# Mixer A's sink as a further column of a head's scores, and a row's maximum turned in sign by ScalarE, in a two-layer fp32 encoder

## The chip, the cores and the metric

The kernel runs on one core of one Trainium2 chip, as one program. The metric is the device time of one execution in microseconds (us). Five engines matter: TensorE (PE in the profile; its weight loads are listed as PEld), VectorE (DVE), ScalarE (ACT), GpSimd (POOL), and the sync engine (SP), from whose queue every DMA of this kernel is issued.

## The reference

Two layers over 256 tokens of width 2048, all in fp32. Each layer has a mixer sub-layer and a gated MLP with a convolution of width 3. The part that the change touches is the softmax of the mixer's two attentions, 8 heads each of width 128:

```python
# mixer A: window attention with a learned sink per head
s = jnp.where(mask, q @ k.T * HEAD_DIM ** -0.5, NEG_INF)
m = jnp.maximum(jnp.max(s, axis=-1, keepdims=True), snk)
p = jnp.exp(s - m)
p = p / (jnp.sum(p, axis=-1, keepdims=True) + jnp.exp(snk - m))
o = p @ v
# mixer B: neighbourhood attention with a 2-D relative bias, a plain softmax without a sink
p = jax.nn.softmax(s + bias)
```

Around it: `h @ w_in` gives q, k, v and two gates; `w_proj_a` and `w_proj_b` project the heads' outputs; the gated sum goes through `w_out`; then `w_up`, the convolution, silu times value, and `w_down`. An adaLN product (`silu(c) @ ada_w`) gives shifts, scales and gates.

## The kernel before, in words

**Products in three parts.** Every fp32 product is made of three fp32r matmuls: each operand is split into a high part and a rest, and high x high, high x rest, rest x high are summed in PSUM. `feature_block` (L314 to L316) does this for one 128x128 block of weights against 256 tokens: the weights `hl` are stationary, the activations are the moving operand, 256 columns (258 where a `Bare` chunk carries two more columns). `tokens` (L377 to L379) does q, k and v the other way round: activations `h` stationary, 512 columns of `hl` moving.

**The stream of weights.** The weights come in units of 1 MB, 16 blocks, in the order of use. For each unit SP issues a DMA into a `raw` buffer, ACT writes the high part of each half (L297), and DVE the rest (L298), into one of four `hl` buffers. DVE also does the adaLN product, one 128x2048 instruction per 1 MB tile of `ada_w` (L226).

**Attention** runs in the background of that stream. A generator per head is advanced by one step at the end of some units. `head_a` and `head_b` take a buffer `p` (tag "p", two buffers) and call `attend`: PE makes the scores `sc` (L607); for each of two halves of the tokens DVE adds the mask (A) or the bias (B, which a DMA has put into `p` itself) and takes the row maximum `m`, begun at the sink for A (L610); DVE turns the sign (`nm`, L615); ACT takes the exponential with its row sum `den` (L618). For A, ACT then makes exp(sink - max) (`es`, L621) and DVE adds it to `den` (L622). DVE takes the reciprocal (L624), ACT scales the rows (L626), PE transposes them (`tp`, L631), the halves of the transpose go to `pT`, and PE multiplies with `v` (`po`, L639).

**GpSimd** does the inverse square roots alone: of q's and k's norms (`qrs`, L441) and of the layer norms (L457).

**Where tiles lie.** Pools are laid out one after another in a partition of SBUF; in the built programs a tile begins at a multiple of 32 bytes. In order: `const` (with `x`), `lay`, `raw`, `hl`, `h`, `ev`, `at` (the attention's buffers: `qn`, `p`, `pT`, and the halves of v, q and k), `sm` (the small tiles: `m`, `nm`, `den`, `es`, `ri`, three buffers each), a padding of 224 bytes, and last `s`, whose seven places hold, by turns, the packed q, k and v, the heads' outputs `oA` and `oB`, the gates `ya` and `gb`, the bare chunks, and the MLP's activations `act`. So the size of `p` and the number of tags in `sm` set where `s` begins. A few tiles are shifted by the code: with `OFF, ROW = 48, 64` (floats), `chunks_of` puts the last chunk of a place 64 bytes further on where there is room, `led` puts chunk 0 of `h` and of `merged` 192 bytes ahead of the rest's phase, `paired` (heads 6 and 7 of `oA`) shifts by 64 bytes. The "phase" of an operand below is its byte address modulo 256, in the built program.

| operand, before | phase |
|---|---|
| stationary `hl` in L314 to L316 | 32 |
| moving `h`, `merged`: chunk 0; the other 15 | 32; 224 |
| moving `act`, `oA`, `oB`: most chunks | 224 |
| moving, the last chunk of `act` in the second and third groups of the MLP, `oB` of head 7, `oA` of heads 6 and 7 | 32 |
| `pT` and the halves of k (moving); the halves of q and v (stationary) | 224; 32 |

The scheduler orders each engine's instructions by its own estimate of the times, so an edit in `attend` shifts neighbouring work by some places.

Of the kernel before, what the change touches and what calls it, by code (L numbers as in the profile page):

```python
# [9 lines left out]
F32 = mybir.dt.float32  # L10
F32R = mybir.dt.float32r
AF = mybir.ActivationFunctionType
ALU = mybir.AluOpType
AX = mybir.AxisListType

P = 128
L = 2
D = 2048
S = 256
# [115 lines left out]
def encoder(ctx: ExitStack, tc: tile.TileContext, a: dict, out: bass.AP):  # L135
    nc = tc.nc
# [14 lines left out]
    at = pool("at", 2)  # L151
    sm = pool("sm", 3)
# [30 lines left out]
    def place(tag, n, dt, name):  # L183
        return sp.tile([P, n, S], dt, name=name, tag=tag)
# [16 lines left out]
    def paired(dt, name):  # L201

        t = ev.tile([P, 2 * S + ROW], dt, name=name, tag="u", bufs=2)
        return t[:, ROW - OFF : ROW - OFF + 2 * S].rearrange("p (a s) -> p a s", a=2)
# [181 lines left out]
    def split(dst, src, scale=None):  # L386

        if scale is None:
            nc.scalar.copy(dst[:, 0], src)
            nc.vector.tensor_tensor(out=dst[:, 1], in0=src, in1=dst[:, 0].bitcast(F32), op=ALU.subtract)  # L390
            return
        nc.scalar.activation(out=dst[:, 0], in_=src, func=AF.Copy, scale=scale)
        nc.vector.scalar_tensor_tensor(
            out=dst[:, 1], in0=src, scalar=scale, in1=dst[:, 0].bitcast(F32), op0=ALU.mult, op1=ALU.subtract
        )
# [192 lines left out]
    def in_halves(src, name, tag, yes):  # L588

        if not yes:  # L590
            return (src,)
        off = {"vh": ROW - OFF, "qh": 0, "kh": OFF}[tag]
        hl = at.tile([P, 2 * S + off], F32R, name=name, tag=tag, bufs=1)[:, off:]
        halves = hl.rearrange("p (i s) -> p i s", i=2) if len(src.shape) == 2 else hl.rearrange("p (i a s) -> p i a s", i=2, a=2)
        split(halves, src)
        return halves[:, 0], halves[:, 1]

    def by(x):

        return ((0, 0), (0, 1), (1, 0))[: 2 * len(x) - 1]  # L600

    def attend(q, k, v, p, mask, scale, sink, o):

        sc = ax.tile([P, 2, S], F32, name="sc", tag="ax")
        for t in range(2):
            for i, j in by(q):
                nc.tensor.matmul(sc[:, t], q[i][:, t * P : (t + 1) * P], k[j], start=i + j == 0, stop=(i, j) == by(q)[-1])  # L607
        m = sm.tile([P, 2], F32, name="m", tag="m")
        for t in range(2):
            nc.vector.tensor_tensor_reduce(  # L610
                out=p[:, t], in0=sc[:, t], in1=mask[:, t], scale=scale, scalar=-3.0e38 if sink is None else sink,
                op0=ALU.add, op1=ALU.max, accum_out=m[:, t : t + 1],
            )
        nm = sm.tile([P, 2], F32, name="nm", tag="nm")
        nc.vector.tensor_scalar(out=nm[:], in0=m[:], scalar1=-1.0, scalar2=None, op0=ALU.mult)  # L615
        den = sm.tile([P, 2], F32, name="den", tag="den")
        for t in range(2):
            nc.scalar.activation(out=p[:, t], in_=p[:, t], func=AF.Exp, bias=nm[:, t : t + 1], accum_out=den[:, t : t + 1])  # L618
        if sink is not None:
            es = sm.tile([P, 2], F32, name="es", tag="es")  # L620
            nc.scalar.activation(out=es[:], in_=nm[:], func=AF.Exp, bias=sink)  # L621
            nc.vector.tensor_tensor(out=den[:], in0=den[:], in1=es[:], op=ALU.add)  # L622
        ri = sm.tile([P, 2], F32, name="ri", tag="ri")
        nc.vector.reciprocal(out=ri[:], in_=den[:])  # L624
        for t in range(2):
            nc.scalar.activation(out=p[:, t], in_=p[:, t], func=AF.Copy, scale=ri[:, t : t + 1])  # L626
        yield
        tp = ax.tile([P, 2, S], F32, name="tp", tag="ax")
        for k in range(2):
            for t in range(2):  # L630
                nc.tensor.transpose(tp[:, k, t * P : (t + 1) * P], p[:, t, k * P : (k + 1) * P], ident[:])  # L631
        pT = at.tile([P, 2, 2, S], F32R, name="pT", tag="pT", bufs=1)
        split(pT, tp[:])
        v = v()
        yield
        po = ax.tile([P, 512], F32, name="po", tag="ax")
        for i, j in by(v):
            for b in range(2):
                nc.tensor.matmul(po[:, :S], v[i][:, b], pT[:, j, b], start=i + j + b == 0, stop=i + b == 2)  # L639
        o = o()  # L640
        nc.scalar.copy(o[:, 0], po[:, :S])
        nc.vector.tensor_tensor(out=o[:, 1], in0=po[:, :S], in1=o[:, 0].bitcast(F32), op=ALU.subtract)
# [93 lines left out]
    def small(l):  # L736

        if l == 0:
            tables.extend((load(a["maskA"], [P, 2, S], "maskA"), load(a["cs"], [P, 2, 2, HALF], "cs")))
        cs = tables[1]  # L740
        gains = load(a["gains"][l], [P, 4], f"gains{l}", lay, tag="gains", bufs=1)
        rg = load(a["rg"][l], [P, 2, ROT], f"rg{l}", lay, tag="rg", bufs=1)
        sink = load(a["sink"][l], [P, HA], f"sink{l}", lay, tag="sink", bufs=1)
        cw = load(a["cw"][l], [P, 2 * FC, 4], f"cw{l}", lay, tag="cw", bufs=1)
        nc.vector.tensor_scalar(out=gains[:, 2:3], in0=gains[:, 2:3], scalar1=SCALE, scalar2=None, op0=ALU.mult)
        rots = []
        for w in range(2):
            rot = lay.tile([P, 4, 2, HALF], F32, name=f"rot{l}_{w}", tag=f"rot{w}", bufs=1)
            for i, (f, g) in enumerate(((0, 0), (1, 1), (0, 1), (1, 0))):
                nc.vector.tensor_tensor(  # L750
                    out=rot[:, i], in0=cs[:, f],
                    in1=rg[:, w, g * HALF : (g + 1) * HALF].unsqueeze(1).broadcast_to([P, 2, HALF]), op=ALU.mult,
                )
            rots.append(rot)

        return gains, sink, cw, rots

    for l in range(L):
# [41 lines left out]
        def head_a(i):  # L800
            g = i // (HA // GA)
            if i >= 6:
                oA.append(paired(F32R, f"oA{l}_{i}"))
            elif i % 2 == 0:
                o = place(("y0", "y1", "y2")[i // 2], 4, F32R, f"oA{l}_{i}")
                oA.extend((o[:, :2], o[:, 2:]))
            q = in_halves(qTa[:, i], f"qA{l}_{i}", "qh", l in SCORES_3)
            if i % (HA // GA) == 0:
                kvs[0] = in_halves(kTa[:, g], f"kA{l}_{g}", "kh", l in SCORES_3)
            k = kvs[0]  # L810
            yield
            p = at.tile([P, 2, S], F32, name="p", tag="p")

            def v():
                if i % (HA // GA) == 0:
                    kvs[1] = in_halves(packs[0][:, 1:4:2, g * HEAD : (g + 1) * HEAD], f"vA{l}_{g}", "vh", True)
                return kvs[1]

            yield from attend(q, k, v, p, tables[0], SCALE, sink[:, i : i + 1], lambda: oA[i])

        def head_b(hb):
            b, i = packs[1 + hb // 4], hb % 4
            v = b[:, 4:8].rearrange("p (t a) s -> p t (a s)", t=2)
            p = at.tile([P, 2, S], F32, name="p", tag="p")
            nc.sync.dma_start(p[:], a["bias"][l, hb])
            q = in_halves(b[:, 8 + i], f"qB{l}_{hb}", "qh", l in SCORES_3)
            k = in_halves(b[:, i], f"kB{l}_{hb}", "kh", l in SCORES_3)
            yield
            yield from attend(
                q, k, lambda: in_halves(v[:, :, i * HEAD : (i + 1) * HEAD], f"vB{l}_{hb}", "vh", True), p, p, 1.0, None,  # L830
                lambda: oB_of(hb),
            )

        def oB_of(hb):
            if hb == 0:
                o = place("a", 12, F32R, f"oB{l}_{hb}")
                oB.extend(o[:, 2 * i : 2 * i + 2] for i in range(6))
            elif hb == 6:
                oB.extend(chunks_of(sp, "b0", 6, f"oB{l}_{hb}", 2))
            return oB[hb]  # L840
# [30 lines left out]
        for pi, (groups, gates) in enumerate(parts):  # L871
            last = pi == len(parts) - 1
            for g, part in enumerate(groups):
                have_h(part)
                pss = st.tokens(h, part)
                if pi == max(0, len(parts) - 2) and g == 0:
                    gains, sink, cw, rots = small(l)
# [56 lines left out]
        for tag in ("y0", "y1", "y2"):  # L934
            t = place(tag, 4, F32, f"gb{l}_{tag}")
            gb += [t[:, i] for i in range(4)]
        for i in range(2):
            t = paired(F32, f"gb{l}_{i}")
# [207 lines left out]
```

## Time and profile before

| | |
|---|---|
| time, three runs | 2666.4, 2667.25, 2667.46 us; median 2667.25 |
| the profiled execution's own time | 2668.06 us |
| its span (first to last instruction) | 2666.3 us |
| busy: PE / DVE / ACT / POOL | 2654.0 / 2099.9 / 1410.1 / 35.8 us |
| matmuls | 21256 |
| moved by DMA | 700.41 MB |

How to read it: a matmul's own duration (some 277 ns) overlaps the next one's, so busy time says only that PE was never without work. What a stretch costs is read from the starts of its matmuls, or from their count in a window: a matmul that begins before the window's edge is counted too, which adds some 2.4 to the count, since one lasts 276 ns and a new one begins each 113 ns.

### The profile page before, as it was taken

The numbers are of one execution on the slowest core, as the hardware profiler recorded it, in microseconds if no ns is written. First come the engines' busy times: TensorE is split into PE (matmuls) and PEld (weight loads), VectorE is DVE, ScalarE is ACT, GpSimd is POOL, SyncE is SP. The second block draws the span as 40 slices with busy tenths as digits, with TensorE's granted clock in tenths as the row PEclk, the third lists the DMA queues.
The fourth block names the chain that finished last, engine by engine and source line by source line (L and its number), as shares of the span: only waits on it lengthen the run. The fifth ranks groups of instructions, "written<-read, shape, count | busy, mean of one in ns | idle before, by whom it ended". The sixth has DMA issues, their size and how long they took to land.

```text
span 2666.3 us, 50840 instructions
## 1 busy us (share of the span) xinstructions
PE 2654.0 (100%) x21256; PEld 2566.7 (96%) x21256; DVE 2099.9 (79%) x2959; ACT 1410.1 (53%) x2284; POOL 35.8 (1%) x25
## 2 busy tenths in 40 slices
PE   9999999999999999999999999999999999999999
PEld 7888899999999999999998889999999999999999
DVE  8898998997987888788886666768888866655664
ACT  5445864446653554355554566554565445544553
POOL 0001100000000000000000000000000000000000
PEclk9999999999999999999999999999999999999999
DMA  9987779885777878788757666666747775555554
GB/s 365 354 328 292 263 280 357 327 313 204 281 291 296 292 293 294 284 298 288 293 215 254 231 236 225 246 256 247 291 167 292 294 256 193 190 192 194 198 192 143
DMA packets 102039, 700.41 MB, mean 263 GB/s; under 512 B 12721, under 2 KB 15025, under 8 KB 17969
## 3 DMA queue, kind: packets, MB, share of 16 engines
q1 hardware_dynamic: 101810, 697.17, 71.2%
q8 instruction: 166, 2.72, 0.4%
q14 instruction: 63, 0.52, 0.1%
HBM read 695.03 MB, written 2.10 MB: 261 GB/s over the span
## 4 chain that ended last, share of the span: by engine, by line
PE 89%; DVE 6%; DMA 2%; ACT 1%; issue 1%; POOL 0%; SPq 0%; DVEq 0%; ACTq 0%
PE ps L314 25%; PE ps L316 25%; PE ps L315 25%; PE ps_t L379 4%; PE ps_t L377 4%; PE ps_t L378 4%; DVE hl L298 2%; DVE aw L226 2%; DMA aw<-in_aw 1%; PE sc L607 1%; ACT hl L297 1%; PE po L639 1%; DMA w<-in_ws 1%; PE tp L631 1%; PE qtp L580 0%
## 5 line engine op out<-in xcount | busy, mean ns | idle before, releaser
L298 DVE TENSOR_TENSOR hl<-w,hl 128x1024 fp32r<-128x1024 f32 x928 | 1127.6, 1222 | 345.6 <-ACT hl L297 342.4
L297 ACT CAST hl<-w 128x1024 fp32r<-128x1024 f32 x928 | 970.0, 1049 | 719.5 <-PE ps L316 504.7
L314 PE MATMUL ps<-h,hl 128*128 128x256 f32 x3328 | 922.1, 277 | 1.3 <-DVE ya L915 0.6
L315 PE MATMUL ps<-h,hl 128*128 128x256 f32 x3328 | 919.9, 276 | 0.0
L316 PE MATMUL ps<-h,hl 128*128 128x256 f32 x3328 | 919.7, 277 | 0.0
L314 PEld LDWEIGHTS ps<-h,hl 128*128 128x128 f32 x3328 | 624.7, 188 | 2.3 <-DVE ya L915 0.8
L315 PEld LDWEIGHTS ps<-h,hl 128*128 128x128 f32 x3328 | 625.3, 188 | 0.3 <-DVE h L470 0.2
L316 PEld LDWEIGHTS ps<-h,hl 128*128 128x128 f32 x3328 | 624.3, 188 | 0.0
L226 DVE CUSTOM_DVE_ANT_0 aw<-aw,cact,ab 128x2048 f32<-128x2048 f32 x189 | 443.5, 2347 | 73.6 <-DMA aw<-in_aw 73.3
L377 PE MATMUL ps_t<-hl,h 128*128 128x512 f32 x576 | 223.2, 392 | 2.6 <-ACT h L469 1.7
L378 PE MATMUL ps_t<-hl,h 128*128 128x512 f32 x576 | 224.9, 391 | 0.3
L379 PE MATMUL ps_t<-hl,h 128*128 128x512 f32 x576 | 224.4, 390 | 0.0
L991 DVE SCALAR_TENSOR_TENSOR u<-ps,cw,u 128x255 f32<-128x255 f32 x304 | 146.1, 481 | 62.0 <-ACT u L989 58.0
L989 ACT ACTIVATE u<-ps,cw 128x256 f32<-128x256 f32 x152 | 85.6, 563 | 171.5 <-PE ps L316 171.3
L316 PE MATMUL ps<-merged,hl 128*128 128x256 f32 x512 | 141.9, 277 | 0.8 <-DVE hl L298 0.8
L314 PE MATMUL ps<-merged,hl 128*128 128x256 f32 x512 | 141.7, 277 | 0.0
L315 PE MATMUL ps<-merged,hl 128*128 128x256 f32 x512 | 141.6, 277 | 0.0
L315 PE MATMUL ps<-act_o,hl 128*128 128x256 f32 x512 | 141.4, 276 | 0.0
L316 PE MATMUL ps<-act_o,hl 128*128 128x256 f32 x512 | 141.3, 276 | 0.0
L314 PE MATMUL ps<-act_o,hl 128*128 128x256 f32 x512 | 141.2, 276 | 0.0
L377 PEld LDWEIGHTS ps_t<-hl,h 128*128 128x128 f32 x576 | 107.9, 188 | 25.9 <-ACT h L469 2.7
L378 PEld LDWEIGHTS ps_t<-hl,h 128*128 128x128 f32 x576 | 108.1, 188 | 24.1 <-DVE hl L298 2.1
(231 smaller groups left out, 4617.6 us busy)
## 6 DMA issues: line engine op xcount, KB each, us to landing
w<-in_ws SPq DMA_DIRECT2D x463, 1024.0 KB, 4.9
aw<-in_aw SPq DMA_DIRECT2D x189, 1024.0 KB, 6.0
p<-in_bias SPq DMA_DIRECT2D x16, 256.0 KB, 3.3
x<-in_xT SPq DMA_DIRECT2D x4, 512.0 KB, 5.3
aw_o<-in_aw SPq DMA_DIRECT2D x2, 1024.0 KB, 12.3
out<-x SPq DMA_DIRECT2D x16, 128.0 KB, 2.7
w<-in_ws SPq DMA_DIRECT2D x2, 512.0 KB, 11.6
aw_b<-in_aw SPq DMA_DIRECT2D x1, 1024.0 KB, 18.4
```

The costliest lines, as they stand in the source:

```text
L226: nc.vector.tensor_tensor_reduce(out=raw[:], in0=raw[:], in1=cact[:], scale=1.0, scalar=ab[:, i : i + 1], op0=ALU.mult, op1=ALU.add, accum ...
L297: nc.scalar.copy(hl[:, 0], r)
L298: nc.vector.tensor_tensor(out=hl[:, 1], in0=r, in1=hl[:, 0].bitcast(F32), op=ALU.subtract)
L314: nc.tensor.matmul(out, hi, act[0], start=first, stop=False)
L315: nc.tensor.matmul(ps[:, :S], hi, act[1], start=False, stop=False)
L316: nc.tensor.matmul(out, lo, act[0], start=False, stop=last)
L377: nc.tensor.matmul(ps[:], xh, hi, start=kc == kcs[0], stop=False)
L378: nc.tensor.matmul(ps[:], xh, lo, start=False, stop=False)
L379: nc.tensor.matmul(ps[:], xl, hi, start=False, stop=kc == kcs[-1])
L607: nc.tensor.matmul(sc[:, t], q[i][:, t * P : (t + 1) * P], k[j], start=i + j == 0, stop=(i, j) == by(q)[-1])
L989: nc.scalar.activation(out=u, in_=ps, func=AF.Identity, scale=w[:, 1:2], bias=w[:, 3:4])
L991: nc.vector.scalar_tensor_tensor(out=u[:, to], in0=ps[:, of], scalar=w[:, j : j + 1], in1=u[:, to], op0=ALU.mult, op1=ALU.add)
```

## The change

For mixer A, `p` gets one column more, and GpSimd writes the head's sink into it ahead of the scores. The exponential then runs over 257 columns, so that the row sum holds exp(sink - max), and `es` with its addition goes. The maximum's sign is turned by ScalarE (a Copy with scale -1) in all heads, in place of VectorE. `p` of mixer B takes the same, wider buffer, and its bias is loaded into the first 256 columns of each half.

```diff
         for t in range(2):
             nc.vector.tensor_tensor_reduce(
-                out=p[:, t], in0=sc[:, t], in1=mask[:, t], scale=scale, scalar=-3.0e38 if sink is None else sink,
+                out=p[:, t, :S], in0=sc[:, t], in1=mask[:, t, :S], scale=scale, scalar=-3.0e38 if sink is None else sink,
                 op0=ALU.add, op1=ALU.max, accum_out=m[:, t : t + 1],
             )
         nm = sm.tile([P, 2], F32, name="nm", tag="nm")
-        nc.vector.tensor_scalar(out=nm[:], in0=m[:], scalar1=-1.0, scalar2=None, op0=ALU.mult)
+        nc.scalar.activation(out=nm[:], in_=m[:], func=AF.Copy, scale=-1.0)
         den = sm.tile([P, 2], F32, name="den", tag="den")
         for t in range(2):
-            nc.scalar.activation(out=p[:, t], in_=p[:, t], func=AF.Exp, bias=nm[:, t : t + 1], accum_out=den[:, t : t + 1])
-        if sink is not None:
-            es = sm.tile([P, 2], F32, name="es", tag="es")
-            nc.scalar.activation(out=es[:], in_=nm[:], func=AF.Exp, bias=sink)
-            nc.vector.tensor_tensor(out=den[:], in0=den[:], in1=es[:], op=ALU.add)
+            n = S if sink is None else S + 1
+            nc.scalar.activation(
+                out=p[:, t, :n], in_=p[:, t, :n], func=AF.Exp, bias=nm[:, t : t + 1], accum_out=den[:, t : t + 1]
+            )
...
-            nc.scalar.activation(out=p[:, t], in_=p[:, t], func=AF.Copy, scale=ri[:, t : t + 1])
+            nc.scalar.activation(out=p[:, t, :S], in_=p[:, t, :S], func=AF.Copy, scale=ri[:, t : t + 1])
...
-            p = at.tile([P, 2, S], F32, name="p", tag="p")
+
+            p = at.tile([P, 2, S + 1], F32, name="p", tag="p")
+            nc.gpsimd.tensor_copy(out=p[:, :, S], in_=sink[:, i : i + 1].broadcast_to([P, 2]))
...
-            p = at.tile([P, 2, S], F32, name="p", tag="p")
-            nc.sync.dma_start(p[:], a["bias"][l, hb])
+            p = at.tile([P, 2, S + 1], F32, name="p", tag="p")
+            nc.sync.dma_start(p[:, :, :S], a["bias"][l, hb])
```

**What it moves in SBUF.** The two `p` buffers grow from 2048 to 2056 bytes each, rounded up to 2080: 64 bytes more. Everything behind them in `at` and `sm` lies 64 bytes further on. `es` had three buffers of 32 bytes; without them `s` begins 96 bytes earlier, 32 in all. In the built programs:

| tile | byte before | byte after | phase before, after |
|---|---|---|---|
| `pT` (moving) | 152032 | 152096 | 224, 32 |
| halves of v, of q (stationary; v's begin 64 bytes into the tile) | 156128, 158240 | 156192, 158304 | 32, 96 |
| halves of k (moving; 192 bytes into the tile) | 160288 | 160352 | 224, 32 |
| places of `s`: b0, y0, a, o, b1 | 163808, 176096, 188384, 200672, 217056 | 163776, 176064, 188352, 200640, 217024 | 224, 192 |

`raw`, `hl`, `h`, `merged`, `x` and `ev` stay where they were. So all moving chunks that lay at 224 in `s` lie at 192, and the shifted last ones of `act` and `oB` at 0 in place of 32; `oA` of heads 6 and 7, in `ev`, stays at 32.

**What it moves in the queues.** DVE in the first two heads of layer 0, before (`sc`, `p`, `m`, `nm`, `den`, `es`, `ri` as above; `sink_996` is layer 0's sink; the ISA rows of L610 are the maximum, those of L226 the adaLN product; `rot` is a table for the next layer):

```order
298 L610 ISA m 128x1
299 L610 ISA p,m<-sc,maskA,sink_996 128x256
300 L610 ISA m 128x1
301 L298 TENSOR_TENSOR hl_45_1_2472<-w_45_2467,hl_45_1_2472 128x1024
302 L615 TENSOR_SCALAR nm<-m 128x2
303 L556 TENSOR_TENSOR qn<-packB_0_224,qrs 128x512 x2
304 L226 ISA aw_37_2640,mod_172<-aw_37_2640,cact,ab_173 128x2048
305 L226 ISA mod_172 128x1
306 L622 TENSOR_TENSOR den<-den,es 128x2
307 L750 TENSOR_TENSOR rot_0_15957<-cs,rg_15950 128x32 x2
308 L624 RECIPROCAL ri<-den 128x2
309 L298 TENSOR_TENSOR hl_46_0_2538<-w_46_2536,hl_46_0_2538 128x1024
```

And after:

```order
298 L610 ISA m 128x1
299 L610 ISA p,m<-sc,maskA,sink_996 128x256
300 L610 ISA m 128x1
301 L298 TENSOR_TENSOR hl_45_1_2470<-w_45_2465,hl_45_1_2470 128x1024
302 L556 TENSOR_TENSOR qn<-packB_0_224,qrs 128x512 x2
303 L226 ISA aw_37_2634,mod_172<-aw_37_2634,cact,ab_173 128x2048
304 L226 ISA mod_172 128x1
305 L623 RECIPROCAL ri<-den 128x2
306 L298 TENSOR_TENSOR hl_46_0_2534<-w_46_2532,hl_46_0_2534 128x1024
```

`nm` and the addition to `den` are gone from DVE's queue, where `nm` stood behind an L298; the table `rot` has moved elsewhere, and the rest is in the same order.

GpSimd's queue from the first layer norm on, before:

```order
10 L457 TENSOR_TENSOR nrs<-ms_in,mhalf 128x2
11 L441 TENSOR_TENSOR qrs<-qss,mhalf 128x4
12 L441 TENSOR_TENSOR qrs<-qss,mhalf 128x8 x6
13 L457 TENSOR_TENSOR nrs<-nss,mhalf 128x2 x2
14 L441 TENSOR_TENSOR qrs<-qss,mhalf 128x4
15 L441 TENSOR_TENSOR qrs<-qss,mhalf 128x8 x6
```

And after (`sink_996` and `sink_15936` are the sinks of the two layers):

```order
10 L457 TENSOR_TENSOR nrs<-ms_in,mhalf 128x2
11 L813 COPY p<-sink_996 128x2 x2
12 L441 TENSOR_TENSOR qrs<-qss,mhalf 128x4
13 L441 TENSOR_TENSOR qrs<-qss,mhalf 128x8 x3
14 L813 COPY p<-sink_996 128x2 x2
15 L441 TENSOR_TENSOR qrs<-qss,mhalf 128x8
16 L813 COPY p<-sink_996 128x2
17 L441 TENSOR_TENSOR qrs<-qss,mhalf 128x8
18 L813 COPY p<-sink_996 128x2 x2
19 L441 TENSOR_TENSOR qrs<-qss,mhalf 128x8
20 L813 COPY p<-sink_996 128x2
21 L813 COPY p<-sink_15936 128x2 x2
```

The copies of the sink stand among the inverse roots of q's and k's norms; from row 14 on a root stands behind copies that need a `p` buffer to be free.

## The prediction

> **What bounds the kernel now.** I read the page first (busy time, clock, chain), then PE in windows of a single stage, then single matmul starts, and last the two attentions.
>
> ```profile
> span 2666.3 us, 50840 instructions
> PE 2654.0 (100%) x21256; PEld 2566.7 (96%) x21256; DVE 2099.9 (79%) x2959; ACT 1410.1 (53%) x2284; POOL 35.8 (1%) x25
> PEclk9999999999999999999999999999999999999999
> PE 89%; DVE 6%; DMA 2%; ACT 1%; issue 1%; POOL 0%; SPq 0%; DVEq 0%; ACTq 0%
> ```
>
> PE has work all the time, at the full granted clock, and is 89% of the chain. So there are two ways to change the time: to change how long PE waits, or how fast one matmul follows another. For the second, the rows of PE alone in three stages of layer 1 (time, busy PE and count; the count in brackets holds some 2.4 matmuls begun before the window, as each lasts 276 ns):
>
> ```profile
> 2096.00:2171.00 75.00, 75.00 (x664) 1.00 0.80 292
> 2450.00:2591.00 141.00, 141.00 (x1242) 1.00 0.55 191
> 2592.00:2662.00 70.00, 70.00 (x617) 1.00 0.45 157
> ```
>
> The first is the down product of the MLP's first group (14 chunks, all moving operands at phase 224): 75.00 / 661.6 = 113.4 ns a matmul. The second is an up product (16 chunks of `h`, chunk 0 at phase 32): 141.00 / 1239.6 = 113.7. The third is the last down product (13 chunks, the last at phase 32): 70.00 / 614.6 = 113.9. The more often a chunk lies at 32, the slower. The single starts show it directly, at the end of three blocks of one chunk at 224, three at 32, and the next at 224 (start in us first):
>
> ```profile
> 2372.24 0.28 PE L314 MATMUL ps<-act_b,hl 128*128 128x256 f32 x1
> ...
> 2373.26 0.28 PE L314 MATMUL ps<-act_b,hl 128*128 128x256 f32 x1
> ...
> 2374.32 0.29 PE L314 MATMUL ps<-act_a,hl 128*128 128x256 f32 x1
> ...
> 2374.68 0.28 PE L314 MATMUL ps<-act_a,hl 128*128 128x256 f32 x1
> ```
>
> Nine starts at 224 take 1.02 us, 113.3 ns each. Nine at 32 take 1.06 us, and the three behind them 0.36 where three take 0.34: 60 ns more for nine, so 6.7 ns each, 120 ns for a matmul at 32. Against three units of 16: 113.3 is 17/16 of 106.7, 120 is 18/16. So the place of the moving operand, with the weights at 32 in all these rows, is worth 5.9% of a matmul's time, and this is what the change moves, besides what it says.
>
> The Trainium skill, page "SBUF — State Buffer", section "Specifications (TRN2)", gives 16-byte lines as what an access pays for, and all phases here (224, 192, 32, 0) are multiples of 16. By that rule no position would cost more than another; the rows above disagree, 1.02 against 1.06 us with its tail, and the measurement decides. What the rule would give is the second rival.
>
> **The change part by part.**
>
> *Operands in `s`, phase 224 to 192.* Those are the 256-column matmuls whose moving chunk lay at 224 in `s` and not in a bare chunk: the MLP's down products, 44 chunks x 16 outputs x 2 layers x 3 = 4224 less the 192 at 32, so 4032; `w_proj_a`, 6 x 16 x 2 x 3 = 576; `w_proj_b`, 7 x 16 x 2 x 3 = 672. In all 5280, a quarter of the matmuls. No row shows phase 192. The ends: nothing, if 192 is as good as 224; 6.7 x 5280 = +35.2 us, if it is as bad as 32; and below nothing, since the 17/16 might itself come from a chunk that begins 32 bytes off a multiple of 64, which 192 is not. A floor for that is the spacing of the transposes of q and k, whose moving operand (`ident`) lies at a multiple of 64:
>
> ```profile
> 281.63 0.33 PE tp L631
> ...
> 286.61 0.87 PE qtp L580 x8
> ...
> 292.54 0.33 PE tp L631
> ```
>
> 0.87 / 8 = 109 ns, so -4.3 x 5280 = -22.7 us. I take half a step, 3.33 ns: a bare product's rest lies at 96 in some places and 224 in others, in one group and one rate (first row below), so the phase seems to count modulo 128; 224 is then 96, 192 is 64, midway between the good 96 and the bad 32. 3.33 x 5280 = +17.6 us. All of it is on the path, for PE has no slack to hide it.
>
> ```profile
> L315 PE MATMUL ps<-bare_b,hl 128*128 128x256 f32 x64 | 18.1, 283 | 0.0
> L315 PE MATMUL ps<-act_o,hl 128*128 128x256 f32 x126 | 34.8, 276 | 0.0
> ```
>
> *Bare chunks, and chunks from 32 to 0.* 1440 matmuls of `Bare` move too; they already last 283 ns against 276, that is 6 to 7 ns late, at 224. Taken at 0; ends -6.7 x 1440 = -9.6 and +9.6 us. The 288 matmuls that go from 32 to 0 already pay 6.7: taken at 0, ends -3.2 (all to the floor of 109) and +1.9. `pT` and the halves of k go from 224 to 32, with 192 + 96 matmuls: 6.7 x 288 = 1.9 us if they pay as the others, nothing if only the distance to the stationary operand counts, which moves by the same 64 bytes. Taken: +1.0. The second half of `p` begins 4 bytes off for the 64 transposes that read it: under 0.4 us at 6.7 each.
>
> *Attention.* Its dense part is in layer 0:
>
> ```profile
> 260.00:400.00 140.00, 138.89 (x944) 125.16 (x943) 135.16 (x277) 105.16 (x265) 12.38 (x5) 1.00 0.73 270
> L615 DVE TENSOR_SCALAR nm<-m x32: 149/160/170, 277.0 to 1775.7; 128x2 f32<-128x2 f32 x32
> L622 DVE TENSOR_TENSOR den<-den,es x16: 147/158/163, 280.5 to 1624.1; 128x2 f32<-128x2 f32 x16
> L621 ACT ACTIVATE es<-nm,sink x16: 278/280/293, 278.2 to 1623.8; 128x2 f32<-128x2 f32 x16
> ACT p L618 <- DVE nm L615: 3.0, 2, 1.6
> ```
>
> DVE is busy for 135.16 of 140 us there, ACT for 105.16, and PE sits idle for 1.1 us in all. Removed from DVE: 32 x 0.160 + 16 x 0.158 = 7.6 us, of which 24 x 0.16 = 3.8 in layer 0. Added to ACT: 32 signs at the price of `es`, 0.28, less 16 `es`: +4.5 us, +2.2 in layer 0. Column 257 of the exponential adds some 2 ns to 500, 32 times. ACT no longer waits for a sign that stood behind an L298 in DVE's queue (the 3.0 us of the last row); behind that wait stood casts of weights (L297), for which DVE's rests and then PE wait. With PE idle for so little, I take -0.5; ends -3.8 (all of DVE's saving) and +2.2 (all of ACT's load). In layer 1 DVE and ACT have more room, and I take nothing; if that cover went, the ends would be the same size again.
>
> *GpSimd's 16 copies.* None is in the trace. The nearest rows are its power of two columns and the root of eight beside busy DVE:
>
> ```profile
> L166 POOL TENSOR_TENSOR early<-early,mhalf 128x2 f32<-128x2 f32 x1 | 0.7, 710 | 0.0
> 246.39 3.72 POOL L441 TENSOR_TENSOR qrs<-qss,mhalf 128x8 f32<-128x8 f32 x1 [12.82 <-DVE qss L440]
> 246.26 2.35 DVE L226 CUSTOM_DVE_ANT_0 aw<-aw,cact,ab 128x2048 f32<-128x2048 f32 x1
> 248.54 1.22 DVE L298 TENSOR_TENSOR hl<-w,hl 128x1024 fp32r<-128x1024 f32 x1
> ```
>
> So 0.1 to 3.7 us each, on an engine that is 99% idle; nearest 0.7. They are written a step before the scores, while PE works on other blocks, and cost nothing as long as that step (some units of weights) covers them. DVE's instructions beside a working GpSimd last 2.35 and 1.22 us, as they do elsewhere, so DVE loses nothing; GpSimd is the one that stretches.
>
> The Trainium skill, "SBUF — State Buffer", section "Who interferes with whom", says that a DVE instruction with two SBUF inputs and a GpSimd one that reads SBUF exclude each other, whichever comes second waiting. By it, DVE would lose up to 16 x 0.7 = 11 us of busy time, an estimate with the trace's 0.7; the rows show no such loss for DVE, and the sum does without it.
>
> *The bias DMA* now lands in two pieces of 1024 bytes per partition:
>
> ```profile
> p<-in_bias SPq DMA_DIRECT2D x16, 256.0 KB, 3.3
> ```
>
> It is issued one step ahead of the scores from the same place in SP's queue; even doubled, 3.3 us lie within that step. Nothing; end +1 us in all.
>
> **The sum.** 17.6 + 1.0 - 0.5 = +18.1 us on the profiled execution's own 2668.06 (span 2666.3 and 1.8 around it): 2686.2. The median of the runs is 0.8 lower: 2685.4, say 2685. That case alone runs from 2680 to 2692.
>
> **The rivals.**
> - *Full step:* 192 is as bad as 32. +35.2 + 1.0 - 0.5: 2703. For it: the one bad phase known costs a whole sixteenth, and nothing between was seen with matmuls of 256 columns. Against: 192 is only 32 bytes off the good one.
> - *Position does not matter here:* 192 is as good as 224, and what is left is the attention's -0.5, with ends of -4 and +3: 2664 to 2670, say 2667. For it: two of the known phases (224 and 96) are alike, so the good region may be wide. This is also the case in which the relief of DVE does nothing, since PE hardly waited for it.
> - *Faster:* a chunk that begins at a multiple of 64 loses the extra sixteenth, down to the 109 ns of the transposes, 2667.25 - 22.7 - 0.5: 2644. It decides as soon as it is worth 1 ns a matmul. For it: 17/16 is what one spoilt line in each 1024 bytes would give. Against: the 512-column matmuls at 224 would then lose a 32nd and not a 16th:
>
> ```profile
> 1469.82 0.39 PE L378 MATMUL ps_t<-hl,h 128*128 128x512 f32 x1
> ...
> 1472.32 0.39 PE L377 MATMUL ps_t<-hl,h 128*128 128x512 f32 x1
> 284.08 0.23 PE ps_t L378
> 284.31 0.23 PE ps_t L379
> 284.55 0.23 PE ps_t L377
> ```
>
>   Eleven starts take 2.50 us, 227 ns each, where 33/32 of twice 106.7 would be 220.
> - *A wait in place of the old one:* in GpSimd's queue a root stands behind copies that wait until the transposes have read a buffer. Transposes of two heads are 10.9 us apart (281.63 to 292.54); three such roots in layer 0 could each hold the norm of q or k for so long, up to 33 us of delay on heads, of which PE, with other blocks at hand, might see a third: 2667.25 - 0.5 + 11, 2678.
>
> **How the numbers follow.** Half step 0.34, full step 0.17, queue 0.02: slower 0.53. No matter: 0.27, which is the chance of no change (0.2%, or 5.3 us, is about what a measurement of this kernel can tell). Faster 0.20. The time is that of the likeliest case, 2685. The range leaves out the faster case's 0.20 and holds the rest: 2661 (the attention's best end with some of the bare chunks' gain) to 2706 (the full step with part of the bare chunks' loss).
>
> **What would show it.** The first window's stage, with `act` at 192, would have 116.7 ns a matmul under the half step, 120 under the full, 113.4 if position does not matter, 109 if aligned chunks are faster, and the second, with `h` unmoved, 113.7 in any case. L315 on `act_o` would last longer than 276 ns. DVE would be some 7.6 us less busy, ACT some 4.5 more, GpSimd's copies some 0.7 us each, and DVE's L298 still 1.22. I am wrong if the down products keep their pace, or if the time lost sits in layer 0's attention.

## The result, and the profile after

| | before | after |
|---|---|---|
| median of 5 runs each, us | 2667.05 (2666.4 to 2667.46) | 2689.05 (2688.77 to 2691.02) |
| ratio, with its 95% interval | | 1.0085 [1.0074, 1.0095] |
| the profiled execution's own time; its span | 2668.06; 2666.3 | 2688.78; 2687.0 |

The change costs 22 us; the forecast was 2685. The page of the kernel after, by the lines that were shown of before:

```profile
span 2687.0 us, 50871 instructions
PE 2675.7 (100%) x21256; PEld 2590.1 (96%) x21256; DVE 2100.3 (78%) x2911; ACT 1412.3 (53%) x2300; POOL 47.3 (2%) x41
PEclk9999999999999999999999999999999999999999
PE 94%; DVE 2%; ACT 1%; DMA 1%; issue 1%; POOL 0%; SPq 0%; ACTq 0%; DVEq 0%
```

The same 21256 matmuls at the same full granted clock keep PE busy for 21.7 us longer, and PE's share of the chain rises from 89% to 94%. The rest of the span, in which PE is idle, goes from 12.3 us (2666.3 less 2654.0) to 11.3 (2687.0 less 2675.7). So PE does not wait more; its matmuls follow one another more slowly. Two windows of PE alone, the first down product and the up product of layer 1, answer to those of before (time, busy and count, clock, DMA share, GB/s):

```profile
2110.00:2185.00 75.00, 75.00 (x641) 1.00 0.78 282
2470.00:2608.00 138.00, 138.00 (x1215) 1.00 0.54 191
```

With 2.4 taken off each count, `act` at phase 192 runs at 75.00 / 638.6 = 117.4 ns a matmul, where it had 113.4 at 224. `h`, which did not move, runs at 138.00 / 1212.6 = 113.8, as before. L315 on `act_o` lasts longer too, 280 ns against 276:

```profile
L315 PE MATMUL ps<-act_o,hl 128*128 128x256 f32 x512 | 143.3, 280 | 0.0
```

Set stage against stage by the starts of the same matmuls in both traces, the two executions part in the stages whose operand lies in `s`: 2.7, 3.1 and 2.4 us in the three down products of each layer, 1.2 us in layer 1's `w_proj_a`, 1.4 and 1.1 in the two `w_proj_b`, 0.8 and 1.2 in the two bare products of the MLP. That is 22.1 us, as the medians say (22.0). Layer 0's `w_proj_a` runs amid the attention and can't be told apart there; where both have ended (the first matmul of `w_proj_b`, 491 us), the kernel after is 0.3 us ahead. The spans differ by less, 20.7 us, because layer 0's `w_out` took 1.8 us longer in the traced execution of before: PE waited there 0.8 us for a cast (L298), and in the trace of after it did not. That wait is not the change's doing: of two kernels below with the instructions of before, before_s192 has it and all_back32 has not.

The attention's rows of after (its dense window; the sign; the copies; DVE's casts; ACT's wait in that window; the bias DMA), each from its own view:

```profile
260.00:400.00 140.00, 138.93 (x940) 125.37 (x939) 134.36 (x252) 106.68 (x281) 17.56 (x13) 1.00 0.72 266
```

```profile
L615 ACT ACTIVATE nm<-m x32: 188/204/224, 275.7 to 1783.7; 128x2 f32<-128x2 f32 x32
```

```profile
L813 POOL COPY p<-sink 128x2 f32<-128x2 f32 x16 | 13.8, 869 | 266.8 <-PE tp L630 115.9 <-DMA sink<-in_sink 88.6 <-ACT hl L297 62.3
```

```profile
L298 DVE TENSOR_TENSOR hl<-w,hl 128x1024 fp32r<-128x1024 f32 x928 | 1129.2, 1222 | 385.4 <-ACT hl L297 382.7
...
p<-in_bias SPq DMA_DIRECT2D x16, 256.0 KB, 3.1
```

```profile
ACT nm L615 <- DVE m L610: 4.1, 4, 1.6
```

In that window DVE is busy 0.8 us less (134.36 against 135.16), ACT 1.5 more (106.68 against 105.16), GpSimd 5.2 more, and PE is idle for 1.07 us against 1.11. ACT, which waited 3.0 us for signs before, now waits 4.1 us for the maxima in their place. The copies do wait for the transposes to free a buffer, 115.9 us in all, but no instruction is listed as waiting for a copy. The bias in two pieces lands in 3.1 us, as fast as in one.

### The profile page after: what moved, and what is told of

It reads as the page before. It is cut to its first block, busy times and chain, and to the rows that moved or that the text cites. A ratio compares the mean times of both kernels' runs of the same rounds, so it can differ in the third digit from the quotient of the medians.

```text
span 2687.0 us, 50871 instructions
## 1 busy us (share of the span) xinstructions
PE 2675.7 (100%) x21256; PEld 2590.1 (96%) x21256; DVE 2100.3 (78%) x2911; ACT 1412.3 (53%) x2300; POOL 47.3 (2%) x41
## 4 chain that ended last, share of the span: by engine, by line
PE 94%; DVE 2%; ACT 1%; DMA 1%; issue 1%; POOL 0%; SPq 0%; ACTq 0%; DVEq 0%
PE ps L314 27%; PE ps L316 27%; PE ps L315 27%; PE ps_t L379 4%; PE ps_t L377 4%; PE ps_t L378 4%; DVE hl L298 1%; PE sc L607 1%; PE po L638 1%; DVE aw L226 1%; ACT hl L297 1%; DMA w<-in_ws 1%; PE tp L630 1%; PE qtp L580 0%; DMA x<-in_xT 0%
## 5 line engine op out<-in xcount | busy, mean ns | idle before, releaser
L298 DVE TENSOR_TENSOR hl<-w,hl 128x1024 fp32r<-128x1024 f32 x928 | 1129.2, 1222 | 385.4 <-ACT hl L297 382.7
L315 PE MATMUL ps<-h,hl 128*128 128x256 f32 x3328 | 920.2, 277 | 0.0
L315 PEld LDWEIGHTS ps<-h,hl 128*128 128x128 f32 x3328 | 625.4, 188 | 0.4 <-DVE h L470 0.2
L226 DVE CUSTOM_DVE_ANT_0 aw<-aw,cact,ab 128x2048 f32<-128x2048 f32 x189 | 443.6, 2348 | 34.0 <-DMA aw<-in_aw 33.4
L377 PE MATMUL ps_t<-hl,h 128*128 128x512 f32 x576 | 223.3, 392 | 2.8 <-ACT h L469 2.1
L379 PE MATMUL ps_t<-hl,h 128*128 128x512 f32 x576 | 224.3, 390 | 0.0
L316 PE MATMUL ps<-act_o,hl 128*128 128x256 f32 x512 | 143.3, 280 | 0.0
L315 PE MATMUL ps<-act_o,hl 128*128 128x256 f32 x512 | 143.3, 280 | 0.0
L314 PE MATMUL ps<-act_o,hl 128*128 128x256 f32 x512 | 143.0, 280 | 0.0
L315 PE MATMUL ps<-merged,hl 128*128 128x256 f32 x512 | 141.5, 276 | 0.0
L377 PEld LDWEIGHTS ps_t<-hl,h 128*128 128x128 f32 x576 | 108.0, 188 | 26.0 <-ACT h L469 3.1
## 6 DMA issues: line engine op xcount, KB each, us to landing
aw_b<-in_aw SPq DMA_DIRECT2D x1, 1024.0 KB, 18.1
```

The lines of the kernel that those rows point to most:

```text
L226: nc.vector.tensor_tensor_reduce(out=raw[:], in0=raw[:], in1=cact[:], scale=1.0, scalar=ab[:, i : i + 1], op0=ALU.mult, op1=ALU.add, accum ...
L298: nc.vector.tensor_tensor(out=hl[:, 1], in0=r, in1=hl[:, 0].bitcast(F32), op=ALU.subtract)
L314: nc.tensor.matmul(out, hi, act[0], start=first, stop=False)
L315: nc.tensor.matmul(ps[:, :S], hi, act[1], start=False, stop=False)
L316: nc.tensor.matmul(out, lo, act[0], start=False, stop=last)
L377: nc.tensor.matmul(ps[:], xh, hi, start=kc == kcs[0], stop=False)
```

## The experiments

**The change without its move in SBUF, and the move without the change.** The first kernel is the changed one with 32 bytes more of padding ahead of `s`, so that `s` lies at 224 again (`pT` and the halves of q, k and v stay where the change put them). The second is the kernel before with 32 bytes less, so that `s` lies at 192.

```diff
 # the changed kernel
-    skip(224)
+    skip(256)
```

> The changed kernel with 256 bytes of padding ahead of the last pool in place of 224: its places lie at phase 224 again, the order of instructions on every engine is that of the changed kernel. Position theory: the 5280 matmuls of down and output projections fall from 117.3 to 113.3 ns, 21 us, and the bare ones lose some 3: 2664 to 2668 us. Rival (the sink copies, the sign on ScalarE, or the new order cost the time): 2687 to 2691 us, as changed.

Measured: 2666.7 us, ratio to before 0.9997 [0.9988, 1.0006]. PE alone in the first down product, and all engines in layer 0's dense window:

```profile
2096.00:2171.00 75.00, 75.00 (x664) 1.00 0.81 298
```

```profile
260.00:400.00 140.00, 138.62 (x941) 124.89 (x940) 134.46 (x252) 106.55 (x281) 18.12 (x13) 1.00 0.73 266
```

75.00 / 661.6 = 113.4: the old pace. In the dense window PE is idle for 1.38 us, where it was 1.11 before and 1.07 after. What the change says it does, the copies, the signs and the dropped `es`, together with the move of `pT` and the halves, is worth between -3.2 and +1.6 us by the interval.

```diff
 # the kernel before
-    skip(224)
+    skip(192)
```

> The kernel before with 192 bytes of padding in place of 224, nothing else: the last pool's places lie at phase 192, as in the changed kernel. Position theory: 5280 x 4.0 ns = 21 us and some 3 for the bare products: 2689 to 2693 us, the first down product at 117.3 ns a matmul. Rival (the work that the change adds costs the time): 2667 us.

Measured: 2689.06 us, ratio 1.008 [1.0067, 1.0094]. The changed kernel took 2689.05; that they agree so closely is chance, as the four runs here lie between 2688.3 and 2690.2.

```profile
2112.00:2187.00 75.00, 75.00 (x642) 1.00 0.77 284
```

75.00 / 639.6 = 117.3. So 32 bytes of padding make the loss alone, and 32 bytes take it back alone.

**Address or distance?** The prediction read the cost off the moving operand's phase with the weights at 32 throughout. In the next two kernels the weights move. In the first, all tiles behind `const` lie 32 bytes earlier: weights at 0, `act` at 192, the distance from the weights to the moving operand unchanged. In the second, the weights that are not streamed through L377 to L379 lie 32 bytes later, at 64, and everything else stays.

```diff
 # the kernel before: all_back32
-    skip(96, const)
+    skip(64, const)
```

> The kernel before with 64 bytes of padding after x in place of 96: every tile behind it lies 32 bytes earlier, so moving operands lie at 192 and 0, weights at 0, and their distances are as before. If only the distance of moving operand and weights counts: 2667 us, 113.3 ns. If the moving operand's own phase counts: 16440 matmuls at 192 cost 4 ns each, 66 us: about 2733 us, or more with those of 512 columns.

```diff
 # the kernel before: hl64
-        at = OFF if streamed else 0
+        at = OFF if streamed else 8
```

> The kernel before, with the halves of the weights 32 bytes further on (phase 64 in place of 32) in all units but those of q, k and v; the moving operands stay at 224. If the distance counts, 224 - 64 = 160 = 192 - 32 as in the changed kernel, now for all 16440 matmuls that had 224 and 32: +4 ns each, about 2733 us. If the moving operand's own phase counts: 2667 us.

Measured: 2666.87 us and 2731.9 us, once each, as the distance would have it (2667 and 2733). PE alone in the down product of the first:

```profile
2096.00:2171.00 75.00, 75.00 (x664) 1.00 0.79 294
```

And in the down and the up product of the second:

```profile
2140.00:2215.00 75.00, 75.00 (x642) 1.00 0.77 283
2510.00:2651.00 141.00, 141.00 (x1198) 1.00 0.52 187
```

`act` at 192 is fast (113.4 ns) once the weights have moved with it, and at 224 slow (117.3) once the weights have moved towards it by 32; `h`, which no padding had touched, goes from 113.7 to 141.00 / 1195.6 = 117.9. So these two runs go by the distance of the moving operand from the weights: 192 is fast, 160 is slow, whichever of the two was moved. The distance is taken modulo 256 from here on: the weights' buffers follow each other at 8448 bytes, 33 x 256, and the pace is the same in all four, so no longer period shows.

**The other distances.** In each of these the padding alone differs from the kernel before, and so `s`, with the weights at 32. They ask two things: does the distance count modulo 128, as the prediction's half step supposed, and is the loss a smooth curve with its worst at 0?

```diff
 # the kernel before; s96, s32, s64, s160
-    skip(224)
+    skip(96)        # 32, 64, 160 in the others
 # s0
-    skip(224)
+    pass
```

> The kernel before with the last pool's places at phase 96 (128 less than before; padding 96). If the distance to the weights counts modulo 128: as before, 2667 us, 113.3 ns. If it counts modulo 256, with the good place at 192 alone: the pace of some other phase, up to 120 ns and 2702 us.

> Places at phase 32, distance 0 from the weights. The single chunks that lay there before cost 6.7 ns a matmul more: 120 ns throughout, 5280 x 6.7 = 35 us: 2702 us.

> Places at phase 0 (no padding), distance -32 from the weights, on the other side of the bad place. By the few chunks that lie at 0 in the changed kernel, some 120 ns a matmul: 2702 us. If the cost grew evenly with the distance from the good place (+4 ns at 32 bytes): 117 to 121 ns.

> The kernel before with the last pool's places at phase 160, distance 128 from the weights. Known so far: distance 192 gives 113.3 ns, 160 gives 117.3, 64 gives 117.8, 0 gives 120.0, 224 gives 118.3. Between 117.3 and 120 ns: 2688 to 2702 us. If the cost counted modulo 128 it would be that of distance 0, 120.0 ns and 2702 us.

> Places at phase 64, distance 32 from the weights. Between its neighbours at 64 (117.8 ns) and 0 (120.0): 118 to 119 ns, 2689 to 2697 us. If the cost counted modulo 128 it would be that of distance 160, 117.3 ns and 2689 us.

The windows of PE alone in the same down product, in that order:

```profile
2108.00:2183.00 75.00, 75.00 (x639) 1.00 0.77 286
```

```profile
2117.00:2192.00 75.00, 75.00 (x627) 1.00 0.74 279
```

```profile
2109.00:2184.00 75.00, 75.00 (x637) 1.00 0.79 289
```

```profile
2111.00:2186.00 75.00, 75.00 (x635) 1.00 0.77 287
```

```profile
2105.00:2180.00 75.00, 75.00 (x645) 1.00 0.76 284
```

| distance, bytes modulo 256 | kernel | ns a matmul, from the starts in this product | time, us |
|---|---|---|---|
| 192 | before | 113.3 | 2667 |
| 160 | before_s192, after | 117.3 | 2689 |
| 128 | s160 | 118.7 | 2693.7 |
| 64 | s96 | 117.8 | 2689.0 |
| 32 | s64 | 116.7 | 2683.9 |
| 0 | s32 | 120.0 | 2701.6 |
| 224 | s0 | 118.3 | 2690.9 |

Distance 96 was not tried. Of the seven, 192 alone is fast. Modulo 128 fell with s96: distance 64 would have to be as good as 192, and it costs 22 us. s32 confirms the 120 ns that the prediction read off nine starts. s0 misses the 120 that was expected from a few chunks and falls into the range of an even growth; s160 lies in its range. s64 misses what was expected: the loss shrinks from 64 to 32 and then jumps at 0, so the curve is not smooth, and these runs give no rule for it. The same product in layer 0 gives the same seven paces to 0.1 ns. Other products need not: in hl64, distance 160 gives 117.3 in `act` and 117.9 in `h`, of which one chunk in 16 lies elsewhere, so a row of the table is the pace of one product. The paces do add up to the times, within 3 us: (120.0 - 113.3) x 5280 = 35.4 us for s32, which lost 34.6 by 2701.6 - 2667.0; (116.7 - 113.3) x 5280 = 18.0 for s64, which lost 16.9.

**Better than before?** If 192 is the one good distance, the few chunks that both kernels shift to phase 32 only cost time, and a kernel with no chunk shifted should gain. It is the changed one with `s` at 224.

```diff
 # the changed kernel: flat_after_s224
-    skip(224)
+    skip(256)
-        at = [2 * S * k + (ROW - OFF if k == n - 1 < room - 1 else 0) for k in range(n)]
+        at = [2 * S * k for k in range(n)]                # chunks_of
-        at = [0] + [OFF + 2 * S * k for k in range(1, KC)]
+        at = [OFF + 2 * S * k for k in range(KC)]         # led: h, merged
-        return t[:, ROW - OFF : ROW - OFF + 2 * S].rearrange("p (a s) -> p a s", a=2)
+        return t[:, : 2 * S].rearrange("p (a s) -> p a s", a=2)   # paired: heads 6, 7 of oA
```

> The changed kernel with padding 256 and, besides, no chunk shifted to phase 32: chunk 0 of h and merged, the last ones of act and oB, and heads 6 and 7 of oA all lie at 224. Theory: the 1200 matmuls that had distance 0 save 6.7 ns each, 8.0 us, and 108 of 512 columns with their stationary h at 32 some 8 ns each, 0.9 us: 2658 us. Rival (a chunk at another phase somewhere keeps the others in step, or the place matters to VectorE and ScalarE): 2667 us or more.

Measured: 2671.68 us, ratio 1.0004 [0.9994, 1.0015]; five runs lie between 2664.2 and 2664.9, six between 2671.7 and 2674.0, and the profile is of one of the six. So neither the median nor the ratio stands for this kernel, and both groups miss the 2658 that was expected. PE alone in layer 0 (the second attention's gate product) and in the down product of layer 1:

```profile
406.00:481.00 75.00, 75.00 (x639) 1.00 0.94 358
2103.00:2178.00 75.00, 75.00 (x665) 1.00 0.80 297
```

The same distance of 192 gives 75.00 / 636.6 = 117.8 ns in the first and 113.2 in the second. In layer 0 the slow pace holds from about 395 to 628 us, through four products. So the distance does not settle the pace: at 192 there are two, and PE can stay in the slow one.

The next two kernels put some shifted chunks back. In flat_o those are heads 6 and 7 of `oA` and the last chunk of `oB`; in flat_mlp also chunk 0 of the mixers' `h` and of `merged`, so that only the MLP is without a shifted chunk.

```diff
 # the changed kernel with skip(256): chunks_of and led; paired as it was
+        at = [2 * S * k + (ROW - OFF if k == n - 1 < room - 1 and name.startswith("oB") else 0) for k in range(n)]
 # flat_o
+        at = [OFF + 2 * S * k for k in range(KC)]
 # flat_mlp
+        at = [OFF * (k > 0 or name.endswith("_1")) + 2 * S * k for k in range(KC)]
```

> As flat_after_s224, but the last chunks of oA (heads 6 and 7) and of oB stay at phase 32; chunk 0 of h and merged and the last ones of act lie at 224. In the flat kernel PE ran at 117.8 ns a matmul from 402 to 628 us of the profiled run at the very positions that give 113.3 later. Theory (two steady paces at one position; a chunk at another phase brings back the faster): the two chunks in the projections restore it after the attentions, 912 matmuls x 6.7 ns and 0.9 us of the 512-column ones are saved: 2660 us, 113.3 ns from 402 us on, runs close to each other. Rival (the slow pace belongs to the flat h and merged of layer 0 themselves): 117.8 ns there again in part of the runs, 2664 to 2674 us.

> Phase 32 only in the mixers: chunk 0 of h (first sub-layer) and of merged, oA, oB; in the MLP (h of the second sub-layer, act) all chunks at 224. 648 matmuls save 6.7 ns, 4.3 us: 2662.5 us, runs close to each other, since the flat MLP ran at 113.33 ns in the flat kernel. If a chunk at 32 is needed in the MLP too: 117.8 ns in some of its stages and 2667 us or more.

flat_o measured 2666.87 us, ratio 1.0004 [0.9988, 1.0021], not the gain that was expected: ten runs lie between 2664.4 and 2669.8, and one, of which there is no trace, at 2689.27. The gate product of layer 0 is fast again:

```profile
406.00:481.00 75.00, 75.00 (x665) 1.00 0.96 365
```

But the `w_out` product of layer 0, all at distance 192, changes its pace at one wait (starts of single matmuls):

```profile
610.82 0.28 PE L316 MATMUL ps<-merged,hl 128*128 128x256 f32 x1
...
611.84 0.28 PE L316 MATMUL ps<-merged,hl 128*128 128x256 f32 x1
...
612.98 0.38 PE L316 MATMUL ps<-merged,hl 128*128 128x256 f32 x1 [0.18 <-DVE hl L298]
613.20 0.28 PE L314 MATMUL ps<-merged,hl 128*128 128x256 f32 x1
...
614.26 0.28 PE L314 MATMUL ps<-merged,hl 128*128 128x256 f32 x1
```

Nine starts take 1.02 us ahead of the wait for a cast and 1.06 behind it: 113.3 ns, then 117.8, and it stays so until this product ends at 624 us. flat_mlp has a wait in the same place, and there chunk 0 of `merged` lies at 32:

```profile
613.03 0.38 PE L316 MATMUL ps<-merged,hl 128*128 128x256 f32 x1 [0.41 <-DVE hl L298]
...
614.08 0.28 PE L315 MATMUL ps<-merged,hl 128*128 128x256 f32 x1
...
615.14 0.28 PE L315 MATMUL ps<-merged,hl 128*128 128x256 f32 x1
...
618.78 0.29 PE L314 MATMUL ps<-merged,hl 128*128 128x256 f32 x1
618.90 0.28 PE L315 MATMUL ps<-merged,hl 128*128 128x256 f32 x1
619.03 0.28 PE L316 MATMUL ps<-merged,hl 128*128 128x256 f32 x1
619.14 0.28 PE L314 MATMUL ps<-merged,hl 128*128 128x256 f32 x1
...
620.16 0.28 PE L314 MATMUL ps<-merged,hl 128*128 128x256 f32 x1
```

Behind the wait nine starts again take 1.06 us. Some 48 matmuls on, about where the next output's chunk 0 comes round, the starts are 0.12 and 0.13 apart, and from 619.14 on nine take 1.02. The kernel before does the same in its own `w_out`: behind a wait, nine starts take 1.06 us ahead of a chunk 0 (617.62 to 618.68) and 1.02 behind it (619.51 to 620.53).

Yet a shifted chunk does not always bring the fast pace. In before_s192, whose `merged` lies as before, a chunk 0 of the same product (at about 619.8, no wait near) ends it; nine starts ahead of it take 1.02 us and nine behind it 1.06, up to the end of the product:

```profile
618.56 0.28 PE L316 MATMUL ps<-merged,hl 128*128 128x256 f32 x1
...
619.58 0.28 PE L316 MATMUL ps<-merged,hl 128*128 128x256 f32 x1
...
620.16 0.28 PE L316 MATMUL ps<-merged,hl 128*128 128x256 f32 x1
...
621.22 0.28 PE L316 MATMUL ps<-merged,hl 128*128 128x256 f32 x1
```

And flat_o returns to the fast pace without one. In layer 1 its second gate product follows the shifted heads 6 and 7, with a few matmuls of the attention between, and is slow from 1712.9 to 1741 us; there six `po`, four `tp` and six `sc` of the attention come in, and behind them it is fast. PE alone on both sides:

```profile
1716.00:1740.00 24.00, 24.00 (x206) 1.00 0.61 215
1744.00:1768.00 24.00, 24.00 (x214) 1.00 0.68 254
```

That is 24.00 / 203.6 = 117.9 ns and 24.00 / 211.6 = 113.4. The first gate product of layer 1 is slow in flat_o from end to end (117.8 ns). Against flat_mlp the two products lose some 3.2 us, most of the 3.4 by which flat_o is behind it.

flat_mlp measured 2663.47 us against 2667.28, ratio 0.9984 [0.9975, 0.9993]; 2662.5 was expected. All its 11 runs lie below all 21 of before (2665.45 at most, 2665.85 at least), so it beats both kernels, by 4 us. Its MLP, down and up product (PE alone), at 113.4 and 141.00 / 1243.6 = 113.4:

```profile
2095.00:2170.00 75.00, 75.00 (x664) 1.00 0.79 292
2450.00:2591.00 141.00, 141.00 (x1246) 1.00 0.55 195
```

So the traces show PE change its pace where its even stream is disturbed, by a wait, by a chunk at another distance or by the attention's matmuls, and in both directions. Not every disturbance does it: behind a wait of 1.2 us for another engine at 784.53, flat_o's down product begins at the fast pace. Which way a disturbance goes, and what in the chip keeps the two paces apart, stays open.

## Why the prediction was right, and where it was not

- **That the move of `s` sets the time** is shown: after_s224 and before_s192 take it away and make it alone. The first window gave 117.4 ns where the half step said 116.7, the full step 120 and no effect 113.4; `h` kept its 113.7.
- **The half step was a little small.** 4.0 ns in place of 3.33, on 5280 matmuls 21.1 us in place of 17.6. The medians differ by 22.0 us, and the spans by 20.7, where 18.1 had been summed.
- **The reason given for the half step was wrong, and that its size came near was luck.** "The phase seems to count modulo 128" rested on the bare product, whose rest was said to lie at 96 in some places and 224 in others of one group. The row shown is the MLP's bare product of layer 1, where the rest of `bare_b` lies at 224 alone (`half` is 320 floats, 1280 bytes); at 96 it lies in the mixer's (288 floats, 1152 bytes), another group, whose L315 on `bare_b` lasts 283 ns as well. That is the slow rate in both, against 276, so it could not show that 96 is as good as 224, and s96 shows that it isn't. That distance 160 lies between the ends is measured; that it lies there for being half-way is not, since 128, 64, 32 and 224 lie there too.
- **Bare chunks, taken at 0:** the MLP's two bare products lose 0.8 and 1.2 us, the mixer's 0.1, inside the ends of 9.6. The chunks from 32 to 0 were not measured apart. The 2.0 us missing here and the 3.5 of the half step, less the 1.0 taken for `pT`, come to 4.5 us, about what the forecast fell short by (2685 against 2689.05).
- **`pT` and k's halves, taken at +1.0:** the distance found above speaks for the other branch, "nothing if only the distance to the stationary operand counts". It is not shown: before_s192 leaves them where they were and after moves them, at the same time, but 1 us is less than the runs scatter by.
- **Attention, -0.5:** not to be told from 0 (-3.2 to +1.6). DVE's busy time fell by 0.9 us at the same position of `s` (2099.9 to 2099.0 in after_s224), not by 7.6. The 7.6 added up durations, but these rows overlap their neighbours in DVE's queue: by the starts and ends in before's trace, they alone cover 4.1 us. The rest is of the size by which executions with one list of DVE instructions differ (2099.0 in after_s224, 2096.6 in flat_o). A sign on ACT lasts 0.20 us and not the 0.28 of `es`, so 32 signs less 16 `es` make 2.0 us in place of 4.5; ACT's busy time rose by 2.2 (1410.1 to 1412.3). The relief that was argued for, ACT no longer waiting for a sign, is not seen: it waits for the maxima instead.
- **GpSimd's queue:** its copies wait for buffers as that rival said, 115.9 us in all, and no time is lost. They last 0.87 us in the mean where 0.7 was taken, and DVE's L298 keeps its 1222 ns. Beside each other, in the order of their starts, GpSimd's rows and then DVE's in after:

```profile
290.25 2.20 POOL L813 COPY p<-sink 128x2 f32<-128x2 f32 x1 [7.57 <-PE tp L630]
...
314.01 2.31 POOL L813 COPY p<-sink 128x2 f32<-128x2 f32 x1 [6.34 <-PE tp L630]
```

```profile
290.06 2.35 DVE L226 CUSTOM_DVE_ANT_0 aw<-aw,cact,ab 128x2048 f32<-128x2048 f32 x1
```

```profile
313.94 2.34 DVE L226 CUSTOM_DVE_ANT_0 aw<-aw,cact,ab 128x2048 f32<-128x2048 f32 x1
```

  Both copies begin behind an adaLN instruction of DVE and end just after it (292.45 against 292.41, 316.32 against 316.28), while DVE keeps its 2.35 us. In all, twelve of the sixteen copies begin behind such an instruction or an L298 and end 0.04 to 0.05 us after it; the other four last 0.18 to 0.19 us. The Trainium skill, "SBUF — State Buffer", section "Who interferes with whom", says that a DVE instruction with two SBUF inputs contends with a GpSimd one that reads SBUF, and that the order of issue decides which of them is blocked; the trace agrees, with GpSimd as the one that comes second. The estimate of 11 us for DVE, drawn from that section in the prediction, charged the wrong engine here; no copy in this trace came first.
- **The 16-byte lines** of the Trainium skill, "SBUF — State Buffer", section "Specifications (TRN2)", on which the second rival went, do not describe this: all distances in the table above are multiples of 32, and the paces range from 113.3 to 120.0 ns; the measurement decides.

## What to carry to other kernels

When an edit changes the size of a buffer, list where every later tile lies before and after, and price the operands that move: here 32 bytes cost 22 us, and the edit itself nothing that could be measured. Tie such layout to the distance between the two operands of a matmul, and measure it, since the neighbours of the good distance (160 and 224) cost 4.0 and 5.0 ns where the worst costs 6.7. Read PE's pace as starts per window, stage by stage: PE was busy for 99% or 100% of the span in every kernel here.

## What the runs showed of the hardware

- With 256 moving columns of fp32r at the full granted clock, one matmul followed another after 113.3 to 120.0 ns in one product, according to the distance between the addresses of the moving operand and of the weights, modulo 256. The Trainium skill, "TensorE: Matmul & The Clock Gate", section "Step-by-step: what each phase is for", says that loading the next weights takes no SBUF bandwidth from the running matmul. In hl64 only the weights moved, by 32 bytes, and the time grew by 65 us (2731.9 against 2667), so here the time of a matmul depends on both operands' addresses together; by what path, no run shows.
- At one distance (192) there are two steady paces, 113.3 and 117.8 ns, in the kernel before as in its variants. PE changed from one to the other at waits, at chunks that lay at another distance and behind the attention's matmuls, in either direction, and once kept the slow one for 230 us.
